# Sums of squares ahead among the matmuls, two pinned products, and a re-ordered final norm in a two-layer decoder trunk

## The chip, the cores and the metric

The kernel runs on one core of a Trainium2 chip. The metric is the device time of one execution in microseconds (us). One core has a TensorE (PE, matmuls; its weight loads are listed apart as PEld), VectorE (DVE), ScalarE (ACT), GpSimd (POOL) and SyncE (SP, which here only issues DMAs).

## The reference

512 tokens with 1024 channels pass one conformer-convolution layer (A) and one sliding-window attention layer (B), each followed by a SwiGLU feed-forward; the end is a norm over channels. Everything is float32.

```python
def rmsnorm(x, g):
    xf = x.astype(jnp.float32)
    xf = xf * lax.rsqrt(jnp.mean(xf * xf, axis=-1, keepdims=True) + EPS)
    return (xf * g.astype(jnp.float32)).astype(x.dtype)

def swiglu_ffn(x, w_up, w_down):
    gate, up = jnp.split(x @ w_up, 2, axis=-1)
    return (jax.nn.silu(gate) * up) @ w_down
...
    for l in range(DEPTH):
        if l < N_A_LAYERS:
            i = l
            h = h + conformer_conv(rmsnorm(h, norm_mix[l]), conv_w_pw1[i], conv_b_pw1[i],
                                   conv_w_dw[i], conv_b_dw[i], conv_ln_g[i], conv_ln_b[i],
                                   conv_w_pw2[i], conv_b_pw2[i])
        else:
...
            h = h + attn @ w_o[j]
        h = h + swiglu_ffn(rmsnorm(h, norm_ffn[l]), ffn_w_up[l], ffn_w_down[l])
    return rmsnorm(h, norm_final)
```

The hidden width of a feed-forward is 2816 (eleven pairs of 256), `EPS` is 1e-6, D is 1024.

## The kernel before, in words

**Weights.** Every large weight matrix is cut into chunks of 128 rows by 1024 columns. SP loads them in the order in which they will be used into six buffers `raw` (L263); ACT rounds each to a short float32 format, `whi` (L299, a CAST); DVE subtracts that from the original and so makes the rest, `wlo` (L302). Activations are split in the same way. A product then takes three matmuls: high by high, high by low, low by high (`mm3`, L388 to L390; L390 is the one that reads `wlo`). A `whi` or `wlo` buffer can be written anew only when PE has read it for the last time.

**Who sets the order.** The functions below say what is to be done; a scheduler puts the instructions of each engine in order by its own timeline. `tc.issue_after(x)` pins what is written inside it behind the instruction x in that order. `stamp[0]` is always the last matmul that `mm3` has written.

**First feed-forward, second half of the tokens.** The tokens are worked on in two halves of 256. For the first three pairs of the second half (`twin`) an activation's high and low part lie side by side, so that one matmul 512 wide does two products, and one 256 wide the third (`mm2`, L420 and L421). A pair takes four chunks of weights, two for each half of the channels (`half`; `which` is 0 for the gate and 1 for the linear branch, m one of two blocks of 128 columns); each chunk multiplies into two of the pair's four PSUM banks.

Between the first and the second half of the channels of the first pair the norm of these tokens is finished (class `Rms`). ACT squares the channels (L495), DVE adds the squares (L499), PE adds over the partitions by a matmul with a column of ones (L511), DVE makes the mean (L513), POOL raises it to the power -1/2 (L516), ACT multiplies an identity matrix with it (L526, twice) and PE spreads the result over all partitions (L540). `step1` is everything up to L526 and is called for this pair at the end of the second chunk (`half` 0, `which` 1). The mean is noted in `biased`, behind which later subtractions L302 are pinned. The banks are then scaled and passed through silu by L644 (ACT) and L645 (DVE) and what follows them. ACT also multiplies the tokens of this half by the norm's gain (L1295 before, L1299 after the change).

**What follows.** The other eight pairs, for all tokens, go in two groups of four through a scheme that needs seven products instead of eight (`SevenPair`). A product has a name such as S1 or A22, two chunks of weights (some of them sums of two chunks that POOL's DMAs have added up in DRAM, L291) and a block of the activations; `take` (L793) writes one product and what is done with its bank.

**Final norm.** At the end the last pair's down projection is made for one block b of 128 tokens at a time, with tokens on the partitions. A block has two halves g of 512 channels; only block 3's second half is done in two pieces of 256. `then` keeps the order in which things are written, apart for each engine: "t" PE, "v" DVE, "s" ACT, "p" POOL. The helpers are `piece` (matmuls L1635; on DVE L1638, which adds the bank, scaled by the feed-forward's norm, to the residual and writes `room`; on ACT the Square L1641 with its sum), `mean` (L1646 from the first sum, L1648 from each further one), `power` (POOL L1653), `weigh` (L1657, the row of gains times `room`, on POOL for blocks 0 to 2 and on DVE for block 3) and `scale` (L1662 on DVE for g = 1, L1664 on ACT for g = 0, each followed by the DMA that writes 128 x 512 results, L1665; by SP, or by ACT for the last block's first half).

Of the kernel before, what the change touches and what calls it, by code (L numbers as in the profile page):

```python
# [211 lines left out]
def hybrid_trunk(ctx: ExitStack, tc: tile.TileContext, xT, W, prm_in, wdw_in, sinks, relb, onehot, fin, lead, out):  # L212
# [419 lines left out]
    def ffn_up(layer, lo, hi, xg, tok, rms, twin=False, plain=None):  # L632
# [40 lines left out]
        pending = []  # L673
        for pair in range(lo, hi):
# [7 lines left out]
            for half in range(2):  # L682
                for which in range(2):
# [4 lines left out]
                    for k, m in order:  # L688
                        sl = slice(m * P, (m + 1) * P)
                        if twin:  # L690
                            mm2(banks[which * 2 + m], (whi[:, k, sl], wlo[:, k, sl]), xg.both(half * 4 + k)[:, :, tok],
                                half == 0 and k == 0, half == 1 and k == 3)
                            continue
# [3 lines left out]
                    if twin and half == 0 and which == 1 or pending and half + which == 0:  # L697
                        rms.step1()
                    if half == 1 and which == 0:
                        for p in pending:  # L700
                            evac(*p)
                        pending = []
            if pair == lo and not twin:
# [69 lines left out]
    def product(key, block, r, opens, between=None):  # L773

        w = [x.rearrange("p (a k c) -> p a k c", a=2, k=4) for x in get_seven(*key)]
        for which in range(2):
            if which and between is not None:
                between()
            for k in range(4):
                mm3(r[:, which], [v[:, which, k, :] for v in w], [block[e][k] for e in range(2)],  # L780
                    opens and which == 0 and k == 0, which == 1 and k == 3, skip_group_check=True)
# [4 lines left out]
    class SevenPair:  # L786
# [6 lines left out]
        def take(self, a):  # L793
# [6 lines left out]
            product((self.kind, self.pair, a), self.rows.block[PARTNER[a]], r, first)  # L800
# [532 lines left out]
    for group in GROUPS0:  # L1333
# [4 lines left out]
        for pair, a in part2_products(group):  # L1338
# [7 lines left out]
            open_pairs[pair].take(a)  # L1346
# [279 lines left out]
    def piece(b, g, i0, i1):  # L1626
# [14 lines left out]
        then("s", lambda: nc.scalar.activation(temp()[:, cols], v, AF.Square, accum_out=s))  # L1641

    def mean(b, n):
        ss = blocks[b][1]
        if n == 0:
            then("v", lambda: nc.vector.tensor_scalar(ss[:, 4:5], ss[:, 0:1], 1.0 / D, EPS, op0=ALU.mult, op1=ALU.add))  # L1646
            return
        then("v", lambda: nc.vector.scalar_tensor_tensor(ss[:, 4 + n:5 + n], ss[:, n:n + 1], 1.0 / D, ss[:, 3 + n:4 + n],  # L1648
                                                         op0=ALU.mult, op1=ALU.add))
# [9 lines left out]
    def scale(b, g):  # L1659
        o, last = blocks[b][0][:, 2 + g], blocks[b][2]  # L1660
        if g:
# [5 lines left out]
    for b in range(NBLK):  # L1667
        blocks.append([quads.tile([P, 4, 512], F32, tag="quad", name=uid("room")),
                       small.tile([P, 8], F32, tag="ss", name=uid("ss")), None])
        if b > 1:  # L1670
            scale(b - 2, 0)
# [15 lines left out]
    piece(ends, 1, 0, 2)  # L1687
    piece(ends, 1, 2, 4)
    weigh(ends, 0, "v", nc.vector.tensor_mul)
# [36 lines left out]
```

## Time and profile before

| what | us |
|---|---|
| three timed runs | 1042.52, 1042.51, 1041.38 |
| their median | 1042.51 |
| profiled execution | 1041.86 |
| its span in the trace | 1040.0 |
| mean granted clock of PE | 0.998 of full speed |

The span runs from the first to the last recorded instruction; the execution's own time is 1.86 us longer. PE is busy in every fortieth of the span at 90% or more except the last one, where it is at 60%.

How to read the rows. In a timeline a row is a start in us from the span's start, the duration of a group, engine, line, operation, output <- inputs, shapes, and how many instructions of one form stand there one after the other (x4); in brackets is the idle time of the engine ahead of it and what ended that. In the list of waits a row names the engine, line and buffers that waited, the instruction that ended it, and the sum, count and mean. The row of a stretch of time has its bounds and, for each engine in turn (PE, PEld, DVE, ACT, POOL, SP), busy time and count, then PE's granted clock, the share of the DMA engines, and GB/s.

### The profile page before, as it was taken

The numbers are of one execution on the slowest core, as the hardware profiler recorded it, in microseconds if no ns is written. First come the engines' busy times: TensorE is split into PE (matmuls) and PEld (weight loads), VectorE is DVE, ScalarE is ACT, GpSimd is POOL, SyncE is SP. The second block draws the span as 40 slices with busy tenths as digits, with TensorE's granted clock in tenths as the row PEclk, the third lists the DMA queues.
The fourth block names the chain that finished last, engine by engine and source line by source line (L and its number), as shares of the span: only waits on it lengthen the run. The fifth ranks groups of instructions, "written<-read, shape, count | busy, mean of one in ns | idle before, by whom it ended". The sixth has DMA issues, their size and how long they took to land.

```text
span 1040.0 us, 17910 instructions
## 1 busy us (share of the span) xinstructions
PE 1029.2 (99%) x6676; PEld 935.0 (90%) x6676; DVE 793.5 (76%) x1241; ACT 603.7 (58%) x1044; POOL 437.1 (42%) x544
## 2 busy tenths in 40 slices
PE   9999999999999999999999999999999999999996
PEld 8888889999989998899888877789989999898995
DVE  3999988997699795487567566678786877869686
ACT  3887796948575552256353555468645545554653
POOL 3999997842121331033234255501460333223134
PEclk9999999999999999999999999999999999999999
DMA  9999847999999999699999987977698897655542
GB/s 357 332 322 261 153 125 232 260 278 229 292 255 309 283 326 288 182 296 344 325 311 260 244 221 205 243 220 221 208 302 286 252 254 212 196 182 187 193 149 81
DMA packets 68243, 256.73 MB, mean 247 GB/s; under 512 B 7835, under 2 KB 14140, under 8 KB 67132
## 3 DMA queue, kind: packets, MB, share of 16 engines
q1 hardware_dynamic: 54044, 204.95, 56.7%
q0 software_dynamic: 13824, 50.34, 26.2%
q8 instruction: 52, 0.85, 0.3%
q10 hardware_dynamic: 288, 0.31, 0.1%
q14 instruction: 35, 0.29, 0.1%
HBM read 250.32 MB, written 105.91 MB: 343 GB/s over the span
## 4 chain that ended last, share of the span: by engine, by line
PE 98%; DVE 0%; DMA 0%; issue 0%; POOL 0%; ACT 0%; POOLq 0%; ACTq 0%
PE bank L388 21%; PE bank L390 21%; PE bank L389 21%; PE bank L945 10%; PE bank L890 9%; PE bank L386 4%; PE bank L420 2%; PE bank L1460 1%; PE bank L1502 1%; PE bank L1489 1%; PE bank L421 1%; PE bank L1043 1%; PE bank L933 1%; PE bank L1635 1%; PE bank L540 0%; PE bank L1581 0%
## 5 line engine op out<-in xcount | busy, mean ns | idle before, releaser
L299 ACT CAST whi<-raw 128x1024 fp32r<-128x1024 f32 x246 | 256.6, 1048 | 278.1 <-PE bank L389 179.4
L302 DVE TENSOR_TENSOR wlo<-raw,whi 128x1024 fp32r<-128x1024 f32 x246 | 316.6, 1295 | 111.2 <-ACT whi L299 110.3
L389 PE MATMUL bank<-quad,whi 128*128 128x256 f32 (+1 forms) x1016 | 315.3, 312 | 0.0
L388 PE MATMUL bank<-quad,whi 128*128 128x256 f32 (+1 forms) x1016 | 315.0, 314 | 0.0
L390 PE MATMUL bank<-quad,wlo 128*128 128x256 f32 (+1 forms) x1016 | 314.4, 312 | 0.0
L388 PEld LDWEIGHTS bank<-quad,whi 128*128 128x128 f32 x1016 | 192.7, 191 | 12.3 <-issue 1.3
L390 PEld LDWEIGHTS bank<-quad,wlo 128*128 128x128 f32 x1016 | 193.1, 191 | 11.5 <-issue 0.4
L389 PEld LDWEIGHTS bank<-quad,whi 128*128 128x128 f32 x1016 | 193.4, 191 | 11.1 <-issue 0.2
L841 POOL TENSOR_TENSOR up<-up 128x512 f32<-128x512 f32 x38 | 71.7, 1887 | 291.0 <-ACT up L838 265.3
L987 POOL TENSOR_TENSOR pr<-pr,pr 128x256 f32<-128x256 f32 x208 | 154.3, 792 | 7.0 <-ACT pr L986 6.9
L388 PE MATMUL bank<-rows,whi 128*128 128x256 f32 x544 | 153.9, 284 | 0.5 <-ACT whi L299 0.3
L389 PE MATMUL bank<-rows,whi 128*128 128x256 f32 x544 | 153.6, 283 | 0.0
L390 PE MATMUL bank<-rows,wlo 128*128 128x256 f32 x544 | 153.4, 283 | 0.0
L994 DVE SCALAR_TENSOR_TENSOR bank<-apad,wdw,bank 128x256 f32<-128x256 f32 x248 | 112.3, 484 | 3.4
L986 ACT ACTIVATE pr<-apad,wdw 128x256 f32<-128x256 f32 x208 | 98.3, 501 | 14.7 <-POOL pr L987 12.9
L388 PEld LDWEIGHTS bank<-rows,whi 128*128 128x128 f32 x544 | 103.5, 191 | 1.5 <-ACT whi L299 0.5
L389 PEld LDWEIGHTS bank<-rows,whi 128*128 128x128 f32 x544 | 103.7, 191 | 0.5 <-issue 0.2
L390 PEld LDWEIGHTS bank<-rows,wlo 128*128 128x128 f32 x544 | 103.6, 191 | 0.0
L945 PE MATMUL bank<-quad,w 128*128 128x256 f32 x448 | 98.7, 380 | 0.0
L945 PEld LDWEIGHTS bank<-quad,w 128*128 128x128 f32 x448 | 84.9, 190 | 11.8 <-DVE bank L994 0.2
L291 POOL DMA_DIRECT2D sum<-in_W_dram x48 | 44.2, 977 | 60.6 <-DVE wlo L302 56.0
L291 POOL DMA_DIRECT2D sum<-sum x48 | 44.9, 975 | 58.7 <-DVE wlo L302 36.5
(231 smaller groups left out, 1518.4 us busy)
## 6 DMA issues: line engine op xcount, KB each, us to landing
raw<-in_W_dram SPq DMA_DIRECT2D x162, 512.0 KB, 5.9
raw<-sum SPq DMA_DIRECT2D x96, 512.0 KB, 4.5
sum<-in_W_dram SPq DMA_DIRECT2D x64, 512.0 KB, 7.8
sum<-in_W_dram POOLq DMA_DIRECT2D x48, 512.0 KB, 8.8
sum<-sum POOLq DMA_DIRECT2D x48, 512.0 KB, 9.5
sum<-in_W_dram SPq DMA_DIRECT2D x4, 4096.0 KB, 34.2
w<-in_W_dram SPq DMA_DIRECT2D x14, 512.0 KB, 9.2
fd<-fs SPq DMA_DIRECT2D x1, 3072.0 KB, 46.3
```

The source lines that it names most:

```text
L291: additions.append(nc.gpsimd.dma_start(summed[c], chunk(c, SUMS[c[2]][1]), accum_op=ALU.add, max_dma_last_dim=4096).ins)
L299: on_act = nc.scalar.copy(hi, src).ins
L302: latest[:] = [on_act, lo_engine[0].tensor_sub(lo, src, f32(hi)).ins]
L388: nc.tensor.matmul(out, w[0], x[0], start=start, stop=False, **kw)
L389: nc.tensor.matmul(out, w[0], x[1], start=False, stop=False, **kw)
L390: stamp[0] = nc.tensor.matmul(out, w[1], x[0], start=False, stop=stop, **kw).ins
L841: pool_op(nc.gpsimd.tensor_mul(gate, gate, c[:, m, :, 1, :]))
L890: nc.tensor.matmul(out, x, w[:, ws], start=first and e == 0 and i == 0, stop=e == 1 and i == 2, skip_group_check=True)
L945: mm = nc.tensor.matmul(self.pb[:, w * W2:(w + 1) * W2], w1_of(ct, w, k), x[k] if x else xg[k][:, tok], start=k == 0, stop=k == KT - 1)
L986: on_act = nc.scalar.mul(pr, a[:, j:j + W2], tap(j))
L987: on_pool = pool_op(nc.gpsimd.tensor_add(pr, acc, pr))
L994: on_dve = nc.vector.scalar_tensor_tensor(yt if i == nd - 1 else c, src, tap(i), c if i else self.shift, op0=ALU.mult, op1=ALU.add)
```

## The change

There are three parts.

1. In the `twin` pairs, `step1` now returns its last matmul L511 (`turn`), and every matmul of the pair written after it, except those of the first bank (`which` = 0 and m = 0), is pinned behind it. The matmuls of the first bank thus come first.
2. In the first group of the scheme with seven products, the second and third product are each pinned behind the last matmul of the product written before them (`after=stamp[0]`).
3. In the final norm the squares are scaled by D^-0.5, so that their sum is the mean already. `mean` is then one addition with one tensor operand; the three sums of block 3 are put together by one addition of a sum to EPS and one addition of the other two. The power of a block comes right behind its second mean, ahead of the next block's products; L1664 and L1662 of block b - 1 are written in the turn of block b, one block sooner for blocks 0 and 1. For the second halves of blocks 2 and 3 the product with the gains is left out as an operation of its own, and DVE does it together with the scaling.

```diff
-        pending = []
+        pending, turn = [], None
...
                         if twin:
-                            mm2(banks[which * 2 + m], (whi[:, k, sl], wlo[:, k, sl]), xg.both(half * 4 + k)[:, :, tok],
-                                half == 0 and k == 0, half == 1 and k == 3)
+                            with tc.issue_after(turn) if turn and which + m else nullcontext():
+                                mm2(banks[which * 2 + m], (whi[:, k, sl], wlo[:, k, sl]), xg.both(half * 4 + k)[:, :, tok],
+                                    half == 0 and k == 0, half == 1 and k == 3)
                             continue
...
                     if twin and half == 0 and which == 1 or pending and half + which == 0:
-                        rms.step1()
+                        turn = rms.step1()
...
+            turn = None
...
-    def product(key, block, r, opens, between=None):
+    def product(key, block, r, opens, between=None, after=None):
...
             for k in range(4):
-                mm3(r[:, which], [v[:, which, k, :] for v in w], [block[e][k] for e in range(2)],
-                    opens and which == 0 and k == 0, which == 1 and k == 3, skip_group_check=True)
+                with tc.issue_after(after) if after else nullcontext():
+                    mm3(r[:, which], [v[:, which, k, :] for v in w], [block[e][k] for e in range(2)],
+                        opens and which == 0 and k == 0, which == 1 and k == 3, skip_group_check=True)
+                after = None
...
-        for pair, a in part2_products(group):
+        for n, (pair, a) in enumerate(part2_products(group)):
...
-            open_pairs[pair].take(a)
+            open_pairs[pair].take(a, stamp[0] if lo0 == GROUPS0[0][0] and 0 < n < 3 else None)
...
-        then("s", lambda: nc.scalar.activation(temp()[:, cols], v, AF.Square, accum_out=s))
+        then("s", lambda: nc.scalar.activation(temp()[:, cols], v, AF.Square, scale=D ** -0.5, accum_out=s))
...
-        if n == 0:
-            then("v", lambda: nc.vector.tensor_scalar(ss[:, 4:5], ss[:, 0:1], 1.0 / D, EPS, op0=ALU.mult, op1=ALU.add))
-            return
-        then("v", lambda: nc.vector.scalar_tensor_tensor(ss[:, 4 + n:5 + n], ss[:, n:n + 1], 1.0 / D, ss[:, 3 + n:4 + n],
-                                                         op0=ALU.mult, op1=ALU.add))
+        then("v", lambda: nc.vector.tensor_scalar(ss[:, 4 + n:5 + n], ss[:, n:n + 1], ss[:, 3 + n:4 + n] if n else EPS, None,
+                                                  op0=ALU.add))
...
-        if g:
+        if g and b > 1:
+            then("v", lambda: nc.vector.scalar_tensor_tensor(o, blocks[b][0][:, 1], last[:, 0:1], gain[:, 512:1024],
+                                                             op0=ALU.mult, op1=ALU.mult))
+        elif g:
             then("v", lambda: nc.vector.tensor_scalar(o, o, last[:, 0:1], None, op0=ALU.mult))
...
-        if b > 1:
-            scale(b - 2, 0)
         piece(b, 0, 0, 4)
         if b:
             mean(b - 1, 1)
-        if b < ends:
-            weigh(b, 0, "p", nc.gpsimd.tensor_mul)
-        if b:
             power(b - 1, 1)
         if b == ends:
             break
+        if b:
+            scale(b - 1, 0)
+        weigh(b, 0, "p", nc.gpsimd.tensor_mul)
         piece(b, 1, 0, 4)
         mean(b, 0)
-        weigh(b, 1, "p", nc.gpsimd.tensor_mul)
-        if b > 1:
-            scale(b - 2, 1)
-    scale(ends - 2, 1)
+        if b < ends - 1:
+            weigh(b, 1, "p", nc.gpsimd.tensor_mul)
+        if b:
+            scale(b - 1, 1)
     piece(ends, 1, 0, 2)
     piece(ends, 1, 2, 4)
+    mean(ends, 0)
     weigh(ends, 0, "v", nc.vector.tensor_mul)
-    for n in range(3):
-        mean(ends, n)
+    ss = blocks[ends][1]
+    then("v", lambda: nc.vector.scalar_tensor_tensor(ss[:, 6:7], ss[:, 2:3], ss[:, 1:2], ss[:, 4:5], op0=ALU.add, op1=ALU.add))
     power(ends, 2)
+    scale(ends - 1, 1)
     scale(ends - 1, 0)
-    weigh(ends, 1, "v", nc.vector.tensor_mul)
-    scale(ends - 1, 1)
     scale(ends, 0)
     scale(ends, 1)
```

What this does to the order of the instructions is shown at three places. Line numbers after the change are a little higher: L1638 becomes L1642, L1646 and L1648 become L1649 (block 3's last sum: L1694), L1653 L1654, L1657 L1658, L1662 L1666, and the scaling together with the gains is L1663.

PE, in the first twin pair, at the second half of its channels; bank576 to bank579 are its four banks, whi581/wlo582 and whi584/wlo585 its third and fourth chunk, quad289 and quad290 the activations of the last four channel tiles. Before:

```order
L421 MATMUL bank577_3161<-quad290_1399,wlo582_3167 128x256
L420 MATMUL bank577_3161<-quad290_1399,wlo582_3167 128x256
L421 MATMUL bank577_3161<-quad290_1399,whi581_3166 128x512
L420 MATMUL bank578_3162<-quad289_1398,whi584_3189 128x512
L511 MATMUL bank586_3209<-ones_c_121,tmp573_3155 128x1 x2
L421 MATMUL bank578_3162<-quad289_1398,wlo585_3190 128x256
L420 MATMUL bank578_3162<-quad290_1399,whi584_3189 128x512
```

And after the change:

```order
L421 MATMUL bank576_3160<-quad290_1399,wlo582_3167 128x256
L420 MATMUL bank576_3160<-quad290_1399,wlo582_3167 128x256
L421 MATMUL bank576_3160<-quad290_1399,whi581_3166 128x512
L511 MATMUL bank586_3209<-ones_c_121,tmp573_3155 128x1 x2
L420 MATMUL bank577_3161<-quad289_1398,whi581_3166 128x512
L421 MATMUL bank577_3161<-quad289_1398,wlo582_3167 128x256
L420 MATMUL bank577_3161<-quad289_1398,whi581_3166 128x512
```

L511 moves 13 matmuls forward: it stood behind the first matmul of bank578 and now stands behind the last of bank576, with 24 matmuls instead of 12 between it and L540. L540 keeps its place: the same matmuls stand ahead of it in both.

PE, in the first group of the scheme with seven products; whi661/wlo662 are the third product's weights, whi641, whi655 and whi658/wlo659 those of products ahead of it. Before:

```order
L388 MATMUL bank638_3517<-quad575_3159,whi641_3521 128x256
L388 MATMUL bank639_3518<-quad575_3159,whi641_3521 128x256
L388 MATMUL bank650_3618<-quad575_3159,whi655_3625 128x256
L388 MATMUL bank651_3619<-quad575_3159,whi655_3625 128x256
L388 MATMUL bank668_3756<-rows616_3370,whi661_3687 128x256
L389 MATMUL bank668_3756<-rows616_3370,whi661_3687 128x256
L390 MATMUL bank664_3724<-quad287_1396,wlo659_3657 128x256
```

After the change, where whi661 is first read:

```order
L390 MATMUL bank651_3619<-quad575_3159,wlo656_3626 128x256
L388 MATMUL bank651_3619<-quad575_3159,whi655_3625 128x256
L389 MATMUL bank651_3619<-quad575_3159,whi655_3625 128x256
L390 MATMUL bank651_3619<-quad575_3159,wlo656_3626 128x256
L388 MATMUL bank668_3756<-rows616_3370,whi661_3687 128x256
L389 MATMUL bank668_3756<-rows616_3370,whi661_3687 128x256
L390 MATMUL bank668_3756<-rows616_3370,wlo662_3688 128x256
```

Before, two matmuls of the third product stood in the middle of the ones ahead of it; now they stand behind them, 66 matmuls later.

DVE, the last instructions of the kernel; room1739, 1745, 1752 and 1759 are blocks 0 to 3, ss their sums, rs1 the results of the power. Before:

```order
L1662 TENSOR_SCALAR room1739_10867<-room1739_10867,rs11749_10906 128x512
L1638 SCALAR_TENSOR_TENSOR room1759_10952<-bank1761_10956,rs1297_7550,h_75 128x512
L1648 SCALAR_TENSOR_TENSOR ss1753_10921<-ss1753_10921 128x1
L1662 TENSOR_SCALAR room1745_10892<-room1745_10892,rs11756_10936 128x512
L1638 SCALAR_TENSOR_TENSOR room1759_10952<-bank1764_10971,rs1297_7550,h_75 128x256
L1638 SCALAR_TENSOR_TENSOR room1759_10952<-bank1766_10981,rs1297_7550,h_75 128x256
L1657 TENSOR_TENSOR room1759_10952<-room1759_10952,gain1717_10731 128x512
L1646 TENSOR_SCALAR ss1760_10953<-ss1760_10953 128x1
L1648 SCALAR_TENSOR_TENSOR ss1760_10953<-ss1760_10953 128x1 x2
L1657 TENSOR_TENSOR room1759_10952<-room1759_10952,gain1717_10731 128x512
L1662 TENSOR_SCALAR room1752_10920<-room1752_10920,rs11763_10967 128x512
L1662 TENSOR_SCALAR room1759_10952<-room1759_10952,rs11768_10995 128x512
```

After the change:

```order
L1642 SCALAR_TENSOR_TENSOR room1752_10924<-bank1757_10942,rs1297_7550,h_75 128x512
L1649 TENSOR_SCALAR ss1753_10925<-ss1753_10925 128x1
L1666 TENSOR_SCALAR room1745_10892<-room1745_10892,rs11756_10937 128x512
L1642 SCALAR_TENSOR_TENSOR room1759_10955<-bank1761_10957,rs1297_7550,h_75 128x512
L1649 TENSOR_SCALAR ss1753_10925<-ss1753_10925 128x1
L1642 SCALAR_TENSOR_TENSOR room1759_10955<-bank1764_10970,rs1297_7550,h_75 128x256
L1642 SCALAR_TENSOR_TENSOR room1759_10955<-bank1766_10980,rs1297_7550,h_75 128x256
L1649 TENSOR_SCALAR ss1760_10956<-ss1760_10956 128x1
L1658 TENSOR_TENSOR room1759_10955<-room1759_10955,gain1717_10731 128x512
L1694 SCALAR_TENSOR_TENSOR ss1760_10956<-ss1760_10956 128x1
L1663 SCALAR_TENSOR_TENSOR room1752_10924<-room1752_10924,rs11763_10968,gain1717_10731 128x512
L1663 SCALAR_TENSOR_TENSOR room1759_10955<-room1759_10955,rs11768_10993,gain1717_10731 128x512
```

The scalings of block 0 and block 1 come one place sooner (block 0's now stands ahead of these rows), the last mean is one TENSOR_SCALAR and one SCALAR_TENSOR_TENSOR, and the last two rows take the place of one product and two scalings. On POOL, the order of products (P) and powers (W) was P P P W P P W P W W and is now P P W P P W P W W.

More of the change, by code (lines that the diff above doesn't have):

```diff
@@ L791, in __init__, with take @@
             self.chains = {}
-        def take(self, a):
+        def take(self, a, after=None):
             c11, c12, c21, c22 = (self.c[:, m, s] for m in range(2) for s in range(2))
@@ L799, in take @@
             r = self.chains[chain]
-            product((self.kind, self.pair, a), self.rows.block[PARTNER[a]], r, first)
+            product((self.kind, self.pair, a), self.rows.block[PARTNER[a]], r, first, after=after)
             if a == "A11":
```

## The prediction

> **What bounds the kernel now.** First the page: busy shares, then the chain that ended last.
>
> ```profile
> PE 1029.2 (99%) x6676; PEld 935.0 (90%) x6676; DVE 793.5 (76%) x1241; ACT 603.7 (58%) x1044; POOL 437.1 (42%) x544
> PE 98%; DVE 0%; DMA 0%; issue 0%; POOL 0%; ACT 0%; POOLq 0%; ACTq 0%
> ```
>
> PE is busy 99% of the span and makes up 98% of the chain. So there are only three kinds of time to win: PE's work itself (the change leaves every matmul in place), the few waits inside PE's run, and what lies before its first and after its last matmul. The view of the waits, taken for PE alone, names the inner ones in question:
>
> ```profile
> PE bank L540 <- ACT tmp L526: 0.7, 1, 0.7
> PE bank L388 <- ACT whi L299: 0.3, 1, 0.3
> ```
>
> Each happens once. The change touches the places of both, and the end behind PE's last matmul. Since PE is the path from one of these places to the next, what each saves adds up at the end, unless another engine holds PE back in between.
>
> **First part: the sums of squares.** The timeline of PE, then of DVE, POOL and ACT:
>
> ```profile
> 281.85 0.40 PE L420 MATMUL bank<-quad,whi 128*128 128x512 f32 x1
> ...
> 283.27 0.40 PE L420 MATMUL bank<-quad,whi 128*128 128x512 f32 x1
> ...
> 285.61 0.50 PE L511 MATMUL bank<-ones_c,tmp 128*128 128x1 f32 x4
> ...
> 287.69 0.40 PE L421 MATMUL bank<-quad,whi 128*128 128x512 f32 x1
> 288.80 0.70 PE L540 MATMUL bank<-tmp,ones_m 128*128 128x256 f32 x2 [0.71 <-ACT tmp L526]
> 289.15 0.58 PE L420 MATMUL bank<-quad,whi 128*128 128x512 f32 x1
> 289.57 0.28 PE L421 MATMUL bank<-quad,wlo 128*128 128x256 f32 x1
> ```
>
> ```profile
> 280.76 0.95 DVE L499 TENSOR_TENSOR tmp<-tmp,tmp 128x256 f32<-128x256 f32 x2
> 286.14 0.16 DVE L513 TENSOR_SCALAR ms<-bank 128x2 f32<-128x2 f32 x1 [4.43 <-PE bank L511]
> 286.22 3.50 DVE L302 TENSOR_TENSOR wlo<-raw,whi 128x1024 fp32r<-128x1024 f32 x3
> ```
>
> ```profile
> 286.39 1.63 POOL L516 TENSOR_TENSOR rs<-ms,mhalf 128x2 f32<-128x2 f32 x1 [9.47 <-DVE ms L513]
> ```
>
> ```profile
> 288.05 0.69 ACT L526 ACTIVATE tmp<-ident,rs 128x128 f32<-128x128 f32 x2 [1.39 <-POOL rs L516]
> ```
>
> The chain is L511 on PE, mean L513 on DVE, power L516 on POOL, diagonal L526 on ACT, and then L540, which spreads it on PE. From 285.61 it needs until 288.74 (288.05 + 0.69), 3.1 us. PE has only until 287.92: the L421 that starts at 287.69 is 512 wide, and a pair of 512 and 256 columns takes 0.355 (four pairs from 281.85 to 283.27), of which the 256 take 0.12 (below), so 0.23 later the next is due.
>
> The change puts L511 behind the first bank's last four pairs, at 283.27: 2.34 earlier. Its input is there (the L499 pair ends at 281.71). L540 stays due at 287.92, since PE's work ahead of it is the same; the chain now ends at 283.27 + 3.1 = 286.4, 1.5 ahead. In the chain 1.63 is a 128x2 power, slow because DVE runs L302 beside it; the new order keeps two L302 behind L513, so I keep 1.63.
>
> L540 started 0.88 after its due time (288.80 against 287.92), and the 0.42 from 289.15 to 289.57 is 0.19 above 0.23. Ends: 0.71, the idle time that the row states, and 1.07, both delays. I take **0.85**, next to the start-to-start value, since the 0.19 may belong to L540 itself.
>
> What is late next? By the new order on ACT the cast of whi604 stands behind L526, four L1299 and two L644, on DVE wlo605 behind two L645. I put the cast's end near 289.5 and wlo605 near 290.7; PE asks for them behind L540 and 32 matmuls at 0.176, about 294.3. It is hidden by PE's other products, with 3.6 to spare. POOL's DMA issues behind the power move ahead with it, at no cost.
>
> **Second part: the held product.** PE, then ACT:
>
> ```profile
> 323.48 0.64 PE L388 MATMUL bank<-quad,whi 128*128 128x256 f32 x4
> 324.42 0.38 PE L388 MATMUL bank<-rows,whi 128*128 128x256 f32 x1 [0.30 <-ACT whi L299]
> 324.64 0.28 PE L389 MATMUL bank<-rows,whi 128*128 128x256 f32 x1
> ```
>
> ```profile
> 323.32 1.05 ACT L299 CAST whi<-raw 128x1024 fp32r<-128x1024 f32 x1 [1.31 <-PE bank L389]
> ```
>
> The four start 0.12 apart ((0.64 - 0.28) / 3). The fifth, due at 323.96, reads whi661, whose cast can only begin when PE has left the buffer, and starts at 324.42: 0.46; the next comes 0.22 later instead of 0.12: 0.10. In the new order these two stand 66 matmuls later, 7.9 us behind, and the L390 that takes their place reads wlo659. Ends: 0.30 (the stated idle time) and 0.56. I take **0.55**. Waiting on `stamp` costs nothing here: it is PE's own order.
>
> Both gains reach the end only if DVE keeps up between them:
>
> ```profile
> 300.00:310.00 10.00, 10.00 (x59) 8.71 (x58) 10.00 (x12) 6.99 (x10) 1.63 (x2) 1.00 1.05 303
> ```
>
> DVE (third of the busy times) and the DMA engines (1.05) are full here. Replaying DVE's new order with the rows' durations gives wlo659 near 322.1, when PE would ask for it at about 323.1: 1 us to spare.
>
> **Third part: the final norm.** DVE, POOL and ACT at the end:
>
> ```profile
> 1029.88 0.67 DVE L1662 TENSOR_SCALAR room<-room,rs 128x512 f32<-128x512 f32 x1
> 1030.52 0.75 DVE L1638 SCALAR_TENSOR_TENSOR room<-bank,rs,h 128x512 f32<-128x512 f32 x1
> 1031.18 1.05 DVE L1648 SCALAR_TENSOR_TENSOR ss<-ss 128x1 f32<-128x1 f32 x1
> 1032.16 0.47 DVE L1662 TENSOR_SCALAR room<-room,rs 128x512 f32<-128x512 f32 x1
> 1032.56 0.86 DVE L1638 SCALAR_TENSOR_TENSOR room<-bank,rs,h 128x256 f32<-128x256 f32 x2
> 1033.34 0.68 DVE L1657 TENSOR_TENSOR room<-room,gain 128x512 f32<-128x512 f32 x1
> ...
> 1034.19 0.43 DVE L1648 SCALAR_TENSOR_TENSOR ss<-ss 128x1 f32<-128x1 f32 x2
> 1034.54 0.68 DVE L1657 TENSOR_TENSOR room<-room,gain 128x512 f32<-128x512 f32 x1
> 1035.14 1.04 DVE L1662 TENSOR_SCALAR room<-room,rs 128x512 f32<-128x512 f32 x2
> ```
>
> ```profile
> 1024.55 2.65 POOL L1657 TENSOR_TENSOR room<-room,gain 128x512 f32<-128x512 f32 x2 [2.38 <-DVE ss L1646]
> 1027.16 0.57 POOL L1653 TENSOR_TENSOR rs<-ss,mhalf 128x1 f32<-128x1 f32 x1
> 1027.72 2.54 POOL L1657 TENSOR_TENSOR room<-room,gain 128x512 f32<-128x512 f32 x2
> ...
> 1030.93 1.28 POOL L1657 TENSOR_TENSOR room<-room,gain 128x512 f32<-128x512 f32 x1
> ...
> 1034.70 0.95 POOL L1653 TENSOR_TENSOR rs<-ss,mhalf 128x1 f32<-128x1 f32 x1 [1.66 <-DVE ss L1648]
> ```
>
> ```profile
> 1033.54 0.40 ACT L1641 ACTIVATE tmp<-room 128x256 f32<-128x256 f32 x1
> ...
> 1035.69 0.72 ACT L1664 ACTIVATE room<-room,rs 128x512 f32<-128x512 f32 x1 [1.05 <-POOL rs L1653]
> 1036.44 0.35 ACTq L1665 DMA_DIRECT2D out_dram<-room  x1
> ```
>
> A 128x1 L1648 takes 1.05 and ends at 1032.23, when POOL's product ends (1030.93 + 1.28 = 1032.21). So DVE and POOL exclude each other, and the last two pieces of the sum stand behind that, from 1032.56. L1662 does it too: 0.67 at 1029.88, beside the second product of 1027.72 (ends 1030.26), against 0.47 when POOL is free. The new mean has one tensor, so it waits no more; the product of the third block's second half leaves POOL.
>
> But the new scalings of blocks 0 and 1 on DVE fall on POOL's products. By the rows' durations POOL runs: product to 1025.87, power 0.57, product to 1027.80, then DVE's first scaling (0.3), product to 1029.4, power to 1029.95, product to 1031.2. DVE's second scaling wants 1030.0, just behind the power: it waits until 1031.2 and ends at 1031.5. Behind it on DVE stands the last block's first piece (1030.52 so far), then at 1031.48; 0.66 and 0.06 later, at 1032.20, the two 256-wide pieces: 0.36 sooner than 1032.56. ACT's three squares then run close together, so the last starts about 1033.30, 0.24 sooner than 1033.54. Behind it stood two means one after the other (1034.19 to 1034.54); now it is one, and DVE's next large operation starts about 1033.95, **0.59** sooner than 1034.54. That operation again runs beside the last power (0.95 instead of 0.57), so the power, L1664 and the last write keep the 0.59.
>
> By the Trainium skill, "SBUF — State Buffer", section "Who interferes with whom", a DVE instruction with two SBUF inputs or in a two-port mode and a GpSimd instruction lock each other out, and the one that issues first goes on. By that rule the trace agrees in the 1.05, and both new scalings are at risk; it does not say who is first when a product ends.
>
> The last write lands late:
>
> ```profile
> out_dram<-room SPq DMA_DIRECT2D x7, 256.0 KB, 2.0
> out_dram<-room ACTq DMA_DIRECT2D x1, 256.0 KB, 2.6
> ```
>
> One write of the three that crowded in at the end goes earlier; ends 0 and 0.6, I take 0.15, near the row's own 2.6, as two still go together. The DVE's last scaling becomes a 0.68 operation instead of 0.5, hidden beside L1664's 0.72.
>
> **Sum.** 0.85 + 0.55 + 0.59 + 0.15 = 2.14. The profiled execution took 1041.86 (span 1040.0 and 1.86 around it), so 1039.7. The median of the runs is 0.65 above it, 1042.51, which makes **1040.4**.
>
> **Rivals.**
> 1. DVE's second scaling gets in ahead of POOL's product at 1029.95. Then the 256-wide pieces go when PE delivers them, the tail gains about 1.36, the sum 2.9: 1039.6. Against it: POOL goes from a power to the next product without a gap (1027.16 + 0.57 to 1027.72), while DVE must first hear of it.
> 2. POOL keeps going at 1027.80 too, and the first scaling waits for two products. All of DVE's end moves back: by the same steps the tail loses 0.17, the sum is 1.2 to 1.4: 1041.2. Against it: at 1032.21 and 1030.26 the waiting DVE operation got in as the product ended.
> 3. The gain on PE is given back, since DVE and DMA are full from 300 on: if wlo659 or the raw weights come 1 to 2 us later than replayed, PE waits there. That leaves the tail: 0.75, 1041.8. Against it: before the change neither made PE wait there.
> 4. Slower: the whi604 cast, put behind L526 on ACT, now hangs on the power. Each us that the power comes later than 3.6 us behind its replayed end (285.7) stops PE at 294.3 for as long; it outweighs everything above 5.7 us, and at 8 us the time is 1044.8. For it: POOL's power already takes 1.63 instead of 0.57. Against: nothing in these rows holds POOL longer than 2.65.
> That the order isn't what the words say is excluded by the order of the built program.
>
> **Chances.** Forecast 0.55, rivals in turn 0.18, 0.11, 0.10, 0.06. About 0.2% (2.1 us) is what a measurement of this kernel can tell from no change; the forecast lies right at it, and I give 0.32 of its 0.55 to faster. Faster: 0.32 + 0.18 = 0.50; same: 0.23 + 0.11 + 0.10 = 0.44; slower 0.06. The range, from rival 1 with 0.4 of scatter (the runs lie up to 1.1 apart) to rival 3: 1039.2 to 1041.8.
>
> **What would show it.** Right: no wait of PE at L540 and none for whi at the product behind it, L516 near 284 and again 1.6 long; no 128x1 operation of DVE longer than 0.2; L1666 about 1.5 long near 1030; the last write issued 0.6 sooner after PE's last matmul. Wrong: new waits of PE on wlo or whi between 290 and 330, or a first scaling over 1.5 long.

## The result and the profile after

The changed kernel takes 1040.49 us (median of 20 runs, 1039.24 to 1041.66) against 1042.45 (20 runs, 1041.38 to 1042.65): ratio 0.9983, 95% interval 0.9977 to 0.9989, or 1.1 to 2.4 us less. The forecast was 1040.4. The change is thus clear of noise, but at 0.17% it lies below the 0.2% that the prediction took as the limit between faster and same; it had given 0.50 to faster and 0.44 to same. The profiled execution took 1039.24 with a span of 1037.4; that is 2.62 less than the one before, and 0.54 of it has nothing to do with the change, as the table below shows.

The waits of PE after the change (engine, buffers and line that waited, who ended it: sum, times, and the longest, which is what the last number of such a row is):

```profile
PE bank L473 <- POOL ones_m L470: 1.0, 1, 1.0
PE bank L937 <- DVE quad L909: 0.3, 1, 0.3
PE bank L388 <- DVE up L826: 0.2, 1, 0.2
```

Of the list before, the waits at L540 (0.7) and for `whi` (0.3) are gone, and none has come in their place. The sums of squares in the timelines of DVE, PE, POOL and ACT:

```profile
280.22 0.95 DVE L499 TENSOR_TENSOR tmp<-tmp,tmp 128x256 f32<-128x256 f32 x2
283.26 0.16 DVE L513 TENSOR_SCALAR ms<-bank 128x2 f32<-128x2 f32 x1 [2.10 <-PE bank L511]
```

```profile
282.72 0.50 PE L511 MATMUL bank<-ones_c,tmp 128*128 128x1 f32 x4
...
287.37 0.59 PE L540 MATMUL bank<-tmp,ones_m 128*128 128x256 f32 x2
287.61 0.58 PE L420 MATMUL bank<-quad,whi 128*128 128x512 f32 x1
288.03 0.28 PE L421 MATMUL bank<-quad,wlo 128*128 128x256 f32 x1
```

```profile
283.51 1.63 POOL L516 TENSOR_TENSOR rs<-ms,mhalf 128x2 f32<-128x2 f32 x1 [7.13 <-DVE ms L513]
```

```profile
285.17 0.69 ACT L526 ACTIVATE tmp<-ident,rs 128x128 f32<-128x128 f32 x2 [2.69 <-POOL rs L516]
```

From L511 the chain takes 3.1 us as before (282.72 to 285.86), but PE now comes to L540 only at 287.37, 1.5 later, and does not stop.

The end of the kernel, on DVE, POOL, ACT and PE; behind them PE's last row of before, which the prediction did not show:

```profile
1027.89 1.47 DVE L1666 TENSOR_SCALAR room<-room,rs 128x512 f32<-128x512 f32 x1
1029.28 0.74 DVE L1642 SCALAR_TENSOR_TENSOR room<-bank,rs,h 128x512 f32<-128x512 f32 x1
1029.94 0.20 DVE L1649 TENSOR_SCALAR ss<-ss 128x1 f32<-128x1 f32 x1
1030.07 0.86 DVE L1642 SCALAR_TENSOR_TENSOR room<-bank,rs,h 128x256 f32<-128x256 f32 x2
...
1031.67 0.22 DVE L1694 SCALAR_TENSOR_TENSOR ss<-ss 128x1 f32<-128x1 f32 x1
1031.81 0.74 DVE L1663 SCALAR_TENSOR_TENSOR room<-room,rs,gain 128x512 f32<-128x512 f32 x1
```

```profile
1027.79 1.29 POOL L1658 TENSOR_TENSOR room<-room,gain 128x512 f32<-128x512 f32 x1
...
1031.97 0.99 POOL L1654 TENSOR_TENSOR rs<-ss,mhalf 128x1 f32<-128x1 f32 x1 [1.20 <-DVE ss L1694]
```

```profile
1033.74 0.38 ACTq L1669 DMA_DIRECT2D out_dram<-room  x1
```

```profile
1029.64 0.28 PE L1639 MATMUL bank<-whi,hid 128*128 128x256 f32 x1
```

```profile
1031.63 0.28 PE L1635 MATMUL bank<-whi,hid 128*128 128x256 f32 x1
```

PE's last matmul ends at 1029.92 now and at 1031.91 before. The last two pieces of the sum start 0.15 behind that end instead of 0.65, the last write by ACT is issued 3.82 behind it instead of 4.53, and the span ends 7.48 behind it instead of 8.09. (The span is shown to 0.1 us, so a tail is good to 0.05.) That write itself lands no sooner after its issue; its row among the DMAs, with the time to landing at the end, was 2.6 before and is now:

```profile
out_dram<-room ACTq DMA_DIRECT2D x1, 256.0 KB, 2.7
```

Behind the landing about 0.96 us remain until the span ends (3.66 from issue to end less 2.7).

**Where the time came from.** Timed runs scatter by 1 us, and the parts are smaller. So each profile is cut at rows that every kernel has: the start of the last pair of L499 ahead of L511 (the order up to there is the same in all), the start of L540, the start of PE's last matmul, and the end of the span (the tail is counted from the end of that matmul, 0.28 behind its start). The first part is no effect of any edit: over the fourteen profiles it is between 280.22 and 281.85 us. The others repeat within about 0.1 where the instructions are the same. (The kernel before had medians of 1042.23 on the chip of e1 to e4, 1042.36 on those of e5 to e11 and 1042.26 on that of e12. One of e1's eleven runs took 3635.37 and another 1043.98; its median hardly moves by them.)

| kernel | start of last L499 | from there to L540 | from there to the start of PE's last matmul | last write by ACT issued behind PE's end | tail: end of span behind PE's end | median of runs |
|---|---|---|---|---|---|---|
| before | 280.76 | 8.04 | 750.87 | 4.53 | 8.09 | 1042.45 |
| changed | 280.22 | 7.15 | 749.42 | 3.82 | 7.48 | 1040.49 |
| e1 first part | 280.70 | 7.14 | 749.41 | 4.53 | 8.11 | 1041.62 |
| e2 second part | 281.47 | 8.04 | 750.21 | 4.53 | 8.14 | 1042.00 |
| e3 third part | 281.85 | 8.04 | 750.88 | 3.85 | 7.59 | 1041.82 |
| e4 fold | 280.74 | 8.04 | 750.85 | 3.67 | 7.43 | 1041.42 |
| e5 mean | 281.41 | 8.04 | 750.82 | 4.51 | 8.09 | 1042.24 |
| e6 places | 281.77 | 8.05 | 750.79 | 4.32 | 7.86 | 1041.84 |
| e7 scaling first | 281.21 | 7.14 | 749.42 | 3.23 | 6.89 | 1039.58 |
| e8 power free | 280.65 | 7.15 | 749.42 | 3.41 | 7.75 | 1040.49 |
| e9 both | 281.60 | 7.15 | 749.41 | 2.79 | 7.11 | 1039.88 |
| e10 two banks | 281.37 | 7.16 | 749.42 | 3.85 | 7.53 | 1040.42 (one run) |
| e11 three banks | 280.95 | 8.02 | 750.19 | 3.86 | 7.58 | 1040.78 (one run) |
| e12 no row product | 281.33 | 7.15 | 749.43 | 3.49 | 6.46 | 1039.38 |

The change took 1.45 us out of PE's run (750.87 to 749.42) and 0.61 out of the tail (8.09 to 7.48): 2.06, beside 1.96 between the medians. The remaining 0.54 of the profiled difference is the start.

### The profile page after: what moved, and what is told of

Same layout as the page of the kernel before. It is cut to its first block, busy times and chain, and to the rows that moved or that the text cites. A ratio compares the mean times of both kernels' runs of the same rounds, so it can differ in the third digit from the quotient of the medians.

```text
span 1037.4 us, 17906 instructions
## 1 busy us (share of the span) xinstructions
PE 1028.3 (99%) x6676; PEld 934.8 (90%) x6676; DVE 792.6 (76%) x1239; ACT 603.6 (58%) x1044; POOL 435.6 (42%) x543
## 4 chain that ended last, share of the span: by engine, by line
PE 99%; DVE 0%; DMA 0%; issue 0%; POOLq 0%; POOL 0%
PE bank L388 21%; PE bank L390 21%; PE bank L389 21%; PE bank L949 10%; PE bank L894 9%; PE bank L386 4%; PE bank L420 2%; PE bank L1464 1%; PE bank L1506 1%; PE bank L1493 1%; PE bank L421 1%; PE bank L1047 1%; PE bank L1639 1%; PE bank L937 1%; PE bank L540 0%; PE bank L1585 0%
```

## The experiments

The theory behind the prediction, A: three separate waits went, at L540, at the product that reads whi661, and at the end, where POOL's products hold up DVE. Rivals are named with each run.

**One part at a time.** e1 is the first part of the diff alone, e2 the second (`after=stamp[0]`), e3 the third.

> Only the first part (matmuls of the twin pairs pinned behind L511). In the built program every engine's order up to the final norm is that of the changed kernel, the third product included, though nothing pins it here. Theory A (the order decides, not the pin): both waits of PE go, 0.9 at L540 and 0.55 at the product that reads whi661; behind the last L499 of that norm PE's last matmul comes 1.45 sooner than before, the tail behind it is 8.1 as before, time 1042.45 - 1.45 = 1041.0. Theory B (each part takes away its own wait): the wait at L540 goes, that for whi661 (0.3 idle) stays, 1041.55. Theory C (the gain is given back where DVE and the DMA engines are full): new waits of PE on wlo or whi between 290 and 330, 1042.0 or more.

DVE and PE of e1:

```profile
280.70 0.95 DVE L499 TENSOR_TENSOR tmp<-tmp,tmp 128x256 f32<-128x256 f32 x2
```

```profile
287.84 0.59 PE L540 MATMUL bank<-tmp,ones_m 128*128 128x256 f32 x2
...
1030.11 0.28 PE L1637 MATMUL bank<-whi,hid 128*128 128x256 f32 x1
```

PE's run is 749.41 (1030.11 - 280.70), that of the changed kernel, and both waits are off the list: the first part alone wins all that PE wins. The reason is in the order. With L511 moved, the scheduler no longer pulls two matmuls of the third product ahead; the first one that reads whi661 stands where the changed kernel has it. In e1 that matmul starts 50.29 behind the last L499 (330.99 - 280.70), in the changed kernel as well (330.51 - 280.22), before it was 43.66 (324.42 - 280.76). The traces of the two kernels have PE's matmuls in one and the same order throughout, and those of the other engines up to the final norm; so beside the first part the second moves nothing. The first and second part without the third were not run together. The time, 1041.62 against 1042.23 on its chip (ratio 0.9993, 0.9984 to 1.0002), was expected at 1041.0, a gain of 1.45, and showed 0.61; its interval takes in both 1.45 and no gain, so the stretch of the profile decides and not the time. The same holds for e2 to e6, none of whose intervals leaves out 1.

> Only the second part (two products pinned behind the matmul written before them). In the built program one matmul that reads whi661 still stands ahead of its product, 22 matmuls later than before instead of 66. Theory A: 22 matmuls are 2.6 us, more than the 0.46 by which the cast was late, so the wait for whi661 goes and the one at L540 (0.7) stays: PE's last matmul 0.55 sooner, time 1041.9. Theory B (any matmul ahead of its product stops PE, since the cast waits until PE has left the buffer): a wait of about 0.3 stays at the new place, 1042.45.

PE's waits, DVE and PE of e2:

```profile
PE bank L540 <- ACT tmp L526: 0.7, 1, 0.7
```

```profile
281.47 0.95 DVE L499 TENSOR_TENSOR tmp<-tmp,tmp 128x256 f32<-128x256 f32 x2
```

```profile
1031.68 0.28 PE L1637 MATMUL bank<-whi,hid 128*128 128x256 f32 x1
```

The wait for `whi` is gone, that at L540 stays, and PE's run is 750.21, 0.66 shorter than before. The pin is thus a second way to the same gain: 22 matmuls of delay are enough (e2's first matmul that reads whi661 starts at 327.29, 45.82 behind the last L499). e1 and e2 do not add up (1.46 + 0.66), since e1 holds what e2 wins. Theory C of e1 falls with the two lists: no new wait between 290 and 330.

> Only the third part (final norm). Both inner waits of PE as before (0.7 at L540, 0.3 for whi661). Theory A: from PE's last matmul's end to the end of the span 7.5 instead of 8.1, time 1041.85. Theory B (the gain of the tail depends on PE's earlier end, through the writes): tail above 7.8, 1042.2.

Tail 7.59 (7.5 was expected) with PE's run as before (750.88): the third part works by itself, as A had it.

**What in the third part does it.** e4 leaves out the row products and folds them; e5 has only the new `mean` and the scaled square; e6 has the order of powers and scalings of the change with the old mean and all products.

```diff
 e4, on the kernel before
-        weigh(b, 1, "p", nc.gpsimd.tensor_mul)
+        if b < ends - 1:
+            weigh(b, 1, "p", nc.gpsimd.tensor_mul)
...
-    weigh(ends, 1, "v", nc.vector.tensor_mul)
...
+        if g and b > 1:
+            then("v", lambda: nc.vector.scalar_tensor_tensor(o, blocks[b][0][:, 1], last[:, 0:1], gain[:, 512:1024],
+                                                             op0=ALU.mult, op1=ALU.mult))
```

> Of the third part only the folding: products with the gains left out for the second halves of blocks 2 and 3, their scaling done on DVE together with them; mean, powers and scalings stand as before. Theory A (POOL's last product held up DVE): with POOL's product at 1030.93 gone, the mean L1648 of block 2 (1.05 before) is back at 0.2, the scaling of block 1 goes at 1031.3, the last two pieces of the sum at 1031.75 and 1032.2 instead of together at 1032.56; the tail behind PE is 0.7 shorter than 8.1, time 1041.75. Theory B (the old mean with its two tensors is what costs, wherever POOL is): a mean of 0.5 or more stays near the end, tail above 7.9. Theory C (the places of the scalings give the gain): tail 8.0 to 8.1.

DVE, PE and ACT of e4:

```profile
1031.15 0.15 DVE L1648 SCALAR_TENSOR_TENSOR ss<-ss 128x1 f32<-128x1 f32 x1
1031.22 0.48 DVE L1665 TENSOR_SCALAR room<-room,rs 128x512 f32<-128x512 f32 x1
1031.61 0.87 DVE L1638 SCALAR_TENSOR_TENSOR room<-bank,rs,h 128x256 f32<-128x256 f32 x2
```

```profile
1031.59 0.28 PE L1635 MATMUL bank<-whi,hid 128*128 128x256 f32 x1
```

```profile
1035.54 0.38 ACTq L1668 DMA_DIRECT2D out_dram<-room  x1
```

With POOL's product out of the way the old mean takes 0.15 instead of 1.05, and the pieces start 0.26 ahead of PE's end (1031.87). The tail is 7.43: the folding alone wins all that the third part wins.

```diff
 e5, on the kernel before
-        then("s", lambda: nc.scalar.activation(temp()[:, cols], v, AF.Square, accum_out=s))
+        then("s", lambda: nc.scalar.activation(temp()[:, cols], v, AF.Square, scale=D ** -0.5, accum_out=s))
...
+        then("v", lambda: nc.vector.tensor_scalar(ss[:, 4 + n:5 + n], ss[:, n:n + 1], ss[:, 3 + n:4 + n] if n else EPS, None,
+                                                  op0=ALU.add))
```

> Of the third part only the new mean (squares scaled, sums added by an operation with one tensor); products, powers and scalings stand as before. The tail is the time from the end of PE's last matmul to the end of the span, 8.1 before. Theory A (POOL's product is what holds DVE, whichever operation meets it): the mean of block 2 takes 0.2 instead of 1.05, but the scaling of block 1 behind it meets the same product and gets in when that ends; the last two pieces start at the same distance from PE's end as before, within 0.1; tail 8.0 to 8.1. Theory B (the old mean is what costs): the last pieces go when PE delivers them, tail 7.3.

DVE and POOL of e5:

```profile
1031.79 0.20 DVE L1645 TENSOR_SCALAR ss<-ss 128x1 f32<-128x1 f32 x1
1031.91 1.20 DVE L1659 TENSOR_SCALAR room<-room,rs 128x512 f32<-128x512 f32 x1
1033.03 0.86 DVE L1638 SCALAR_TENSOR_TENSOR room<-bank,rs,h 128x256 f32<-128x256 f32 x2
```

```profile
1031.54 1.29 POOL L1654 TENSOR_TENSOR room<-room,gain 128x512 f32<-128x512 f32 x1
```

The new mean goes through beside the product (0.20), but the scaling behind it meets the same product and takes 1.20 instead of 0.47: the wait has only moved one instruction on, and the tail is 8.09 as before. B falls.

> Of the third part only the places: powers and scalings in the order of the changed kernel, with the old mean with two tensors and all products with the gains. Theory A: the product of block 2's second half still runs on POOL when the last sums are due, DVE's mean L1648 of block 2 waits for it, and the last two pieces start 0.8 behind PE's end instead of 0.65; tail 8.0 to 8.4. Theory C (the places give the gain): tail 7.5.

e6 missed what was expected: tail 7.86, not 8.0 to 8.4. The pieces start 0.64 behind PE's end, as before; the last write is issued 4.32 instead of 4.53 behind PE's end. By the order, the 0.2 comes from block 3's first mean, which now stands ahead of the product; that was not tried by itself. C (7.5) falls as well.

**Who comes first on the way of POOL and DVE.** e7 to e9 and e12 are edits on the changed kernel.

```diff
 e7: weigh(2, 0) is written behind scale(1, 1), and made to wait for it
+        if b == ends - 1:
+            weigh(b, 0, "p", nc.gpsimd.tensor_mul)
+            tc.add_manual_dep(order["p"], order["v"].name,
+                              mybir.DependencyInfo(mybir.DependencyClass.Sync, mybir.DependencyReason.DATA), reason="turn")
```

> The changed kernel, with POOL's product of block 2 made to wait until DVE has scaled block 1's second half (in the changed kernel that scaling took 1.47 and ended as the product did). Theory A (the two exclude each other, and who comes first decides): the scaling takes 0.5 or less, the sums' last two pieces come when PE delivers them, about 0.5 sooner; the last write is issued 3.4 behind PE's end instead of 3.82, tail 7.0 instead of 7.48. Theory B (the 1.47 is long but nothing hangs on it): tail 7.4 to 7.5.

DVE, PE and ACT of e7:

```profile
1028.88 0.48 DVE L1666 TENSOR_SCALAR room<-room,rs 128x512 f32<-128x512 f32 x1
...
1030.37 1.05 DVE L1642 SCALAR_TENSOR_TENSOR room<-bank,rs,h 128x256 f32<-128x256 f32 x2
```

```profile
1030.63 0.28 PE L1639 MATMUL bank<-whi,hid 128*128 128x256 f32 x1
```

```profile
1034.14 0.38 ACTq L1669 DMA_DIRECT2D out_dram<-room  x1
```

0.48 instead of 1.47; the two pieces now start 0.54 ahead of PE's end (1030.91) and end 0.51 behind it instead of 1.01. The tail is 6.89, and the time 1039.58 (ratio to before 0.9974, 0.9963 to 0.9984). So the scaling's 1.47 was on the path of the changed kernel.

```diff
 e8, and with e7's edit e9
     power(ends, 2)
-    scale(ends - 1, 1)
     scale(ends - 1, 0)
     scale(ends, 0)
     scale(ends, 1)
+    scale(ends - 1, 1)
```

> The changed kernel, with the scaling of block 2's second half on DVE moved behind that of block 3, so that no operation of DVE runs beside the last power. Theory A (the last power took 0.99 because it waited for the scaling beside it): the power takes 0.57, the last scaling on ACT and its write come 0.42 sooner, 3.4 behind PE's end; block 2's write becomes the last one, 0.75 behind it on DVE; tail 6.9 to 7.4. Theory B (0.99 is the power's own time at this place): the power stays at 0.95 or more, and block 2's later write makes the tail 7.6 or more.

POOL and DVE of e8:

```profile
1032.43 0.55 POOL L1654 TENSOR_TENSOR rs<-ss,mhalf 128x1 f32<-128x1 f32 x1 [1.20 <-DVE ss L1694]
```

```profile
1033.01 1.42 DVE L1663 SCALAR_TENSOR_TENSOR room<-room,rs,gain 128x512 f32<-128x512 f32 x2 [0.66 <-POOL rs L1654]
```

The power is 0.55 instead of 0.99 and ACT's write 0.41 sooner, as A had it; but the tail grew to 7.75 where 6.9 to 7.4 was expected. Block 2's result now comes last, from DVE at 1034.43, 0.7 behind the two writes of block 3. A was right on the power and wrong on the end; the tail that B named (7.6 or more) came, but by block 2's later write and not by the power.

> The changed kernel with both edits: POOL's product of block 2 behind DVE's scaling of block 1, and DVE's scaling of block 2 behind that of block 3. Theory A: the two gains add up, since the first moves the last sum and the second the power behind it; last write of block 3 issued 2.95 behind PE's end, tail 6.4 to 6.8 instead of 7.48; time 0.7 to 1.0 below the changed kernel's 1040.5. Theory B (the writes at the end are the bound, they only crowd together): tail 7.0 or more.

Tail 7.11, time 1039.88, against 6.4 to 6.8 expected: ACT's write goes at 2.79, but the write of block 2 is again the last. Worse than e7 alone, and B's "7.0 or more" holds.

```diff
 e12, on e7
     mean(ends, 0)
-    weigh(ends, 0, "v", nc.vector.tensor_mul)
+    scale(ends - 1, 1)
...
     power(ends, 2)
-    scale(ends - 1, 1)
     scale(ends - 1, 0)
-    scale(ends, 0)
     scale(ends, 1)
+    scale(ends, 0)
...
-        if g and b > 1:
+        if g and b > 1 or b == ends:
...
```

> The kernel with POOL's product of block 2 behind DVE's scaling of block 1 (tail 6.89), and with block 3's first half folded as the others: no product of its own ahead of the last sum, block 2's scaling in its place, and behind the last power DVE does both halves of block 3, one after the other (0.75 each). Nothing runs beside the last power, and each write is issued about 0.75 from the next. Theory A (a write takes 3.66 from issue to end only where another starts beside it, and about 0.7 less alone): the power takes 0.57 and starts 1.35 to 1.45 behind PE's end, the last write is issued 3.5 behind it, tail 6.4 to 6.6. Theory B (3.66 is the write's own time): tail 7.1 to 7.2.

POOL, ACT and PE of e12:

```profile
1032.49 0.55 POOL L1654 TENSOR_TENSOR rs<-ss,mhalf 128x1 f32<-128x1 f32 x1 [1.06 <-DVE ss L1699]
```

```profile
1034.53 0.35 ACTq L1669 DMA_DIRECT2D out_dram<-room  x1
```

```profile
1030.76 0.28 PE L1639 MATMUL bank<-whi,hid 128*128 128x256 f32 x1
```

Tail 6.46. The last write is issued later than in e7 (3.49 behind PE's end, not 3.23), but from there to the end it is 2.97 instead of 3.66 (e7: 1037.8 - 1034.14), as theory A had it: in e7 SP issues a write within 0.03 of it, in e12 the nearest is 0.67 ahead. This is the fastest kernel of the study: 1039.38, ratio to before 0.9972 (0.9961 to 0.9983); the tail is 1.02 shorter than the changed kernel's 7.48, and the medians stand 1.11 apart (1040.49 and 1039.38), though the two intervals still meet (0.9977 to 0.9989 there).

**How far L511 has to move.** In the changed kernel the matmuls behind L511 are those with `which + m` above 0. e10 pins only those with `which`, e11 only those with both.

```diff
-                            with tc.issue_after(turn) if turn and which + m else nullcontext():
+                            with tc.issue_after(turn) if turn and which else nullcontext():
```

> The changed kernel with L511 pinned behind two of the four banks instead of one, so 8 matmuls or 1.4 us later. Theory A (a chain of 3.1 us from L511 to L540, hidden by PE's work between them): the cover shrinks from 4.65 to 3.2, the chain still fits; wait of PE at L540 0 to 0.15; from the last L499 to PE's last matmul 749.4 to 749.6. Theory B (any work behind L511 is worth as much: the gain is in proportion to the distance): half of the 0.9 is lost, 749.9.

> The changed kernel with L511 pinned behind three of the four banks, 16 matmuls or 2.8 us later. Theory A: the cover is 1.8 against a chain of 3.1, PE waits about 1.2 to 1.3 at L540, more than the 0.7 before the change; from the last L499 to PE's last matmul 750.6 to 750.8. Theory B (the wait at L540 comes from ACT's or POOL's queue at that time, not from L511's place): a wait of 0.3 or less.

PE in e10, then PE's wait in e11:

```profile
285.29 0.50 PE L511 MATMUL bank<-ones_c,tmp 128*128 128x1 f32 x4
...
288.53 0.66 PE L540 MATMUL bank<-tmp,ones_m 128*128 128x256 f32 x2
```

```profile
PE bank L540 <- ACT tmp L526: 0.7, 1, 0.7
```

In e10 L511 starts 3.92 behind L499 instead of 2.50, and L540 comes 3.24 behind it without a wait: the chain just fits, and nothing is lost, so the gain is not in proportion to the distance (B falls). e11 missed its numbers, since its pin left L511 where it stood before the change (4.82 behind L499 against 4.85), not 16 but 13 matmuls back; there the wait is 0.7 again and PE's run 750.19. On PE it amounts to the second part without the first. With e10 it shows that L511's place makes the wait; what a place later than the old one costs was not measured.

## Why the prediction held, point by point

Term by term the forecast of 0.85 + 0.55 + 0.59 + 0.15 = 2.14 became 0.79 + 0.66 + 0.71 - 0.10 = 2.06. The mechanism held in the first three terms; that the sum is so close is in part luck, since the two that came out larger make up for the last, which has the wrong sign.

- **What bounds the kernel.** Right: what PE's waits and the tail lost came off the end, 2.06 of 2.14 forecast.
- **Sums of squares, 0.85.** L540 comes 0.89 sooner, between the two ends that were set (0.71 and 1.07). The 0.19 left open there belongs to L540 itself: after the change, too, 0.42 lie between the two rows behind it (287.61 and 288.03). At the end 0.79 is left of it (e11 against the changed kernel: 750.19 - 749.42 = 0.77; 1.45 less e2's 0.66 = 0.79). The chain moved as replayed: L516 again 1.63 long. Rival 4 didn't come: the cast of whi604 behind L526 starts at 287.89 and ends 8.72 behind the last L499, just as replayed (289.5 against 280.76), and PE doesn't wait. How much later it could come was not tried: in e10, where L526 is 1.4 later, the scheduler put this cast ahead of it.
- **Held product, 0.55.** Right as to the wait, 0.10 too small against its own upper end of 0.56 (0.66 in e2; where the rest comes from stays open), and wrong as to which edit wins it: it was put under the second part of the change, and e1 shows that the first part alone makes the scheduler leave the product where it belongs. Beside the first part the second changes nothing.
- **DVE full between.** No wait of PE on `wlo` or `whi` came between 290 and 330 in any kernel with the first part, and PE's run kept the gain (749.42): rival 3 is out.
- **Final norm, 0.59.** The first scaling took 0.98 from 1025.18 and ended at 1026.16, when POOL was still in the second of the two products that end at 1027.30: it did not wait for both, so rival 2 is out. The second met POOL's product as forecast (1.47 for "about 1.5"), the last write is issued 0.71 sooner, 0.12 more than the step gave, as the pieces start 0.50 and not 0.36 sooner. Of the two causes that the step named, the product that leaves POOL is the one (e4); the mean that waits no more gains nothing by itself (e5), and the new places take some of it back, through the 1.47 (e7). Rival 1, which needed DVE to get in first, was built as e7 and has a tail shorter by 1.20 than before; its price was put at 1.36.
- **Last write, 0.15.** The term with the wrong sign: from the last write's issue to the end it is 3.66 now (1037.4 - 1033.74) and was 3.56 (1040.0 - 1036.44), and the landing, 2.7 for 2.6, agrees. The step counted the writes and not their distance. Before, SP's last write was issued at 1036.21, 0.23 ahead of ACT's; now DVE's last operation takes 0.75 beside ACT's 0.72, and SP issues at 1033.77, 0.03 behind ACT. In e1, e2, e5 and e6 the two are 0.23 to 0.24 apart, too, and the span ends 3.5 to 3.6 behind ACT's issue; in e3, e4, e7, e10 and e11 they are 0.03 apart, and it is 3.7 to 3.8. e12, with 0.67 between the last two, has 2.97.

## What to carry to other kernels

When an edit pins one thing, look at what the scheduler does to the rest before crediting a second pin: the gain may be in the order already. It may also go again: in e10, with L511 eight matmuls further back, the first matmul that reads whi661 stands 44 matmuls sooner than in the changed kernel, in spite of the second pin. Where DVE and POOL share the work of a tail, it is the long product that has to move, be folded into the next operation or be made to wait its turn; making the small operation in its way cheaper only hands the wait to the next one. And when parts of a change are smaller than the scatter of the runs, cut the profile at rows that both kernels have and compare the pieces.

## What the runs showed of the hardware

- A POOL product of 1.29 us holds a DVE operation with two 128x1 tensors (1.05 before, 0.15 in e4) and a 128x512 scaling with one (1.20 in e5), but not a 128x1 addition with one tensor (0.20 in e5), and not the sum that reads a bank, as two rows of the changed kernel show, DVE's 0.74 within POOL's pair of products:

```profile
1026.08 0.74 DVE L1642 SCALAR_TENSOR_TENSOR room<-bank,rs,h 128x512 f32<-128x512 f32 x1
```

```profile
1024.59 2.71 POOL L1658 TENSOR_TENSOR room<-room,gain 128x512 f32<-128x512 f32 x2
```

  By the Trainium skill, "SBUF — State Buffer", section "Who interferes with whom", DVE and GpSimd lock each other out where the DVE instruction has two SBUF inputs or is in a two-port mode, and the first to issue goes on; e7 agrees, where DVE first means 0.48 instead of 1.47, and so does the last power, 0.99 with DVE's scaling ahead of it and 0.55 without (e8).
- With two 256 KB writes issued together the span ends 3.66 behind ACT's issue (changed kernel), with one issued 0.7 behind another 2.97 behind it (e12), and with one 0.7 behind two others 3.67 behind the end of the scaling that it waits for (e8: 1038.1 - 1034.43). In the changed kernel 0.96 of this lies behind the landing. So the last write need not start beside another one for the end to come late; two issued 0.7 ahead of it do it, too. Whether it matters which engine issues the last one (ACT in e12, SP in e8) was not tried.
- The time from a fixed row to PE's last matmul, some 750 us, repeats within 0.1 us over the profiles of kernels with the same order on PE; the start up to it varies by 1.6, and so it sets the scatter of the profiled times.
- PE gives a little of a stall back: behind the 0.89 at L540 it loses 0.79 at the end. Why was not tried.
